# A batched trace of matrix products on one core: the first load as two transfers, 16 partitions issued by ScalarE and 112 by SyncE, without a critical section

## The chip, the core and the metric

The kernel runs on one core of a Trainium2 chip. The metric is the device time of one execution in microseconds (us). Before the change it is 706.29 us, the median of three runs (706.15 to 706.38).

The engines are named as in the profile: PE is TensorE (PEld its weight loads), DVE is VectorE, ACT is ScalarE, POOL is GpSimd, SP is SyncE. A transfer is issued by one of ACT, SP or POOL and carried out by the core's 16 DMA engines. Only the transfers that POOL issues change the type on the way (float32 in memory to bfloat16 in SBUF).

## What is computed

```python
prod = np.matmul(a, b)                                  # a, b: 8 x 2176 x 2176, float32
traces = np.diagonal(prod, axis1=1, axis2=2).sum(axis=-1)
```

The trace of a product needs no product: it is the sum over i and j of a[i, j] times b[j, i]. So the kernel has to read both inputs once, 303 MB, turn each `a` over, multiply it element by element with `b` and add up.

## The kernel before

The rows of a matrix are cut in three groups: two of 6 x 128 rows (`a_six`, `b_six`) and one of 5 x 128 rows (`five`). In a group, partition p holds 6 (or 5) neighbouring rows, one behind the other, so each partition is filled by one long contiguous read. For each of the 8 matrices of the batch:

- POOL issues the loads with `fetch` (L168-169): the five rows of `a` (L206), its twelve rows (L209), then the five and twelve rows of `b` (L218, L221). Each waits for the buffer that it writes to. The last matrix of `b` comes in ten pieces (L223 to L226).
- SP waits for the loads of `a` to land and passes this on to PE (the semaphore `moved`, L181 to L190).
- PE transposes 128 x 128 blocks into three PSUM slots (L344, L347); ACT (L236) and DVE (L265) copy them to `at` in SBUF.
- DVE multiplies `at` with the rows of `b` and reduces (L248). For the last matrix PE takes four of the seventeen column blocks (L314, L320), and the ends are added up at L352 and L295.

The first matrix starts in another way. Of the five rows per partition of `a[0]`, the first two (`FIRST` at L39, 4352 float32 elements per partition) are loaded as they are, by a transfer that ACT issues (L172), into memory that belongs to `b_six` and is free at that time (`words`, L166). ACT waits for it (L229) and rounds it to bfloat16 (L230). The other three of the five rows come by POOL's first transfer (L176), the twelve rows by its second (L177). PE starts when POOL's first transfer has landed and the rounding is done (L182 to L185).

ACT's transfer stands in a critical section of the tile framework (L171). On ACT that puts a no-operation, two branches, a semaphore update and a drain around the transfer, and SP waits for its end. Behind it `tc.close()` (L173) ends the framework's part of the program with barriers over all five engines, and only behind these come POOL's transfers and everything else. Another barrier of all five engines stands at the program's start, ahead of the section (L374 in the profile).

Of the kernel before, what the change touches and what calls it, by code (L numbers as in the profile page):

```python
# [22 lines left out]
def kernel(  # L23
# [7 lines left out]
    P = 128  # L31
# [3 lines left out]
    SIX, FIVE = 6, 5  # L35
    TWICE = 2 * SIX
    assert TWICE + FIVE == NT
    LAST = BATCH - 1
    FIRST = 2  # L39
# [76 lines left out]
    def flat(t):  # L116
        return t.rearrange("p r k -> p (r k)")
# [4 lines left out]
    def rows_of(src, start, m, r0, r1):  # L122
        return src[start:start + P * m, :].rearrange("(p r) k -> p (r k)", r=m)[:, r0 * N:r1 * N]
# [21 lines left out]
    def counted(name):  # L145
        return Counted(nc, name)
# [5 lines left out]
    d_a12, d_row = counted("load_a12"), counted("load_row")  # L152
# [12 lines left out]
    gp, act, sp, dve, pe = nc.gpsimd, nc.scalar, nc.sync, nc.vector, nc.tensor  # L165
    words = flat(b_six[:, 0:2 * FIRST, :].bitcast(f32))  # L166
# [1 line left out]
    def fetch(count, dst, src):  # L168
        count.by(gp.dma_start(out=dst, in_=src), 16)  # L169

    with tc.tile_critical(sync_engine=act.engine, no_gpsimd_drain=True):  # L171
        d_row.by(act.dma_start(out=words, in_=rows_of(a[0], TWICE * P, FIVE, 0, FIRST)), 16)  # L172
    tc.close()  # L173
    tc.compile()  # L174

# [20 lines left out]
    for n in range(BATCH):  # L196
        if n == 0:
            gp.wait_ge(zeros.sem, 2)
            for t in (identity32, identity16):
                ready.by(gp.affine_select(  # L200
                    out=t, in_=t, compare_op=mybir.AluOpType.not_equal, fill=1.0, base=0,
# [24 lines left out]
            fetch(d_late[k], piece.dst, piece.src)  # L226


    act.wait_ge(d_row.sem, 16)  # L229
    rounded.by(act.copy(out=flat(five[:, 0:FIRST, :]), in_=words))  # L230
    with nc.Fori(0, BATCH, engines=OrderedEngineSet([act.engine])):
        act.wait_ge(clear, 1).then_inc(clear, -1)  # L232
# [22 lines left out]
    with nc.Fori(  # L255
# [24 lines left out]
        for k, piece in enumerate(pieces[:len(whole) + 1]):  # L280
            if piece is whole[-1]:
                dve.wait_ge(parts.sem, k)
                parts.by(dve.reduce_sum(
                    out=sums[:, taken:taken + 1], in_=late[:, 0:k], axis=mybir.AxisListType.X,
# [11 lines left out]
            out=result[:1, :], in_=total.rearrange("o (b n) -> o b n", n=TAKEN),  # L296
# [5 lines left out]
    with nc.Fori(0, 2, engines=alone) as turn:  # L302
# [54 lines left out]
        out=out.rearrange("(a b) -> a b", a=1), in_=result[:1, :],  # L357
# [32 lines left out]
```

## Time and profile before

| what | before |
|---|---|
| median of three runs | 706.29 us |
| the profiled execution's own time | 706.07 us |
| its span, first to last instruction | 704.7 us |
| granted TensorE clock, mean | 0.647 |
| read from memory, over the span | 303.04 MB, 430 GB/s |
| busy share PE, DVE, ACT, POOL | 29%, 54%, 29%, 4% |
| transfers issued by POOL, share of the 16 DMA engines' span | 99.6% |
| transfer issued by ACT, the same share | 0.8% |

The span leaves out 1.37 us of the execution's own time (706.07 less 704.7), before its first and behind its last instruction. The profiled execution was 0.22 us below the median of the three runs. In the profile a DMA "packet" is one contiguous row of a transfer; a further packet of 4 bytes, one for each DMA engine that took part, counts up the transfer's semaphore. The size of a packet is what it writes: for the transfers of POOL half of what it reads. The share of a DMA queue is the time that its packets took, over 16 engines times the stretch that is looked at. A packet counts where it starts, so short stretches can show a little over 100%.

### The profile page before, as it was taken

What the parts mean: (1) busy time and instruction counts of PE and PEld (TensorE: products, weight loads), DVE (VectorE), ACT (ScalarE), POOL (GpSimd) and SP (SyncE); (2) the same over time, 40 slices, a digit from 0 to 9 for tenths busy, and PEclk for the clock granted to TensorE, in tenths of its full rate; (3) what the DMA queues carried; (4) which work ended last, traced back from release to release, by engine and by line L of the source; (5) the groups of instructions that cost most, each with busy time, mean ns of one, the idle gap of its engine ahead of it and who ended that gap; (6) DMA issues with size and microseconds to landing.
All of it is one profiled execution on the core that took longest, in us unless ns stands there. A gap on an engine that the chain in (4) does not pass through costs nothing. (4 is left out here: it accounts for less than half of the span.)

```text
span 704.7 us, 3807 instructions
## 1 busy us (share of the span) xinstructions
PE 205.4 (29%) x1573; PEld 181.8 (26%) x1573; DVE 382.8 (54%) x101; ACT 207.5 (29%) x162; POOL 25.6 (4%) x47
## 2 busy tenths in 40 slices
PE   0335012450124401344012440134301253014633
PEld 0324012440124401243012430134301243014522
DVE  0105487154871539616397163962639616396388
ACT  2427002470034600346004360044500445005900
POOL 1000000000000000000000000000000000001100
PEclk9759555795567855568556695567855678556955
DMA  9999999999999999999999999999999999999998
GB/s 252 230 200 219 215 228 213 217 225 213 206 216 217 223 213 229 213 213 214 224 209 213 215 228 209 224 222 209 209 229 213 213 211 232 206 215 224 218 206 174
DMA packets 7844, 152.66 MB, mean 217 GB/s; under 512 B 674, under 2 KB 930, under 8 KB 1442
## 3 DMA queue, kind: packets, MB, share of 16 engines
q0 software_dynamic: 7696, 150.41, 99.6%
q10 hardware_dynamic: 144, 2.23, 0.8%
q8 instruction: 1, 0.02, 0.0%
q14 instruction: 1, 0.01, 0.0%
q1 hardware_dynamic: 2, 0.00, 0.0%
HBM read 303.04 MB, written 0.00 MB: 430 GB/s over the span
## 5 line engine op out<-in xcount | busy, mean ns | idle before, releaser
L236 ACT COPY at<-aT 128x1536 bf16<-128x1536 bf16 (+3 forms) x160 | 202.4, 1360 | 452.0 <-ACTq L232 357.9
L248 DVE CUSTOM_DVE_ANT_0 at<-at,rows_b 128x10880 bf16<-128x10880 bf16 (+3 forms) x18 | 278.6, 15484 | 98.1 <-DMA rows_b<-in_b_dram 83.2
L265 DVE COPY at<-aT 128x1536 bf16<-128x1536 bf16 (+1 forms) x48 | 80.1, 1669 | 213.8 <-PE aT L344 163.4
L344 PE MATMUL aT<-identity,rows_b 128*128 128x128 f32 x240 | 54.3, 415 | 369.8 <-PEq L337 282.3
L344 PEld LDWEIGHTS aT<-identity,rows_b 128*128 128x128 f32 x240 | 46.3, 220 | 376.1 <-issue 283.1
L344 PE MATMUL aT<-identity,a_six 128*128 128x128 f32 x576 | 90.7, 320 | 94.9 <-SPq L190 80.8
L344 PEld LDWEIGHTS aT<-identity,a_six 128*128 128x128 f32 x576 | 83.6, 206 | 101.3 <-issue 90.1
L347 PE MATMUL aT<-identity,a_six 128*128 128x128 bf16 x480 | 34.3, 221 | 10.5 <-ACT at L236 9.4
L347 PEld LDWEIGHTS aT<-identity,a_six 128*128 128x128 bf16 x480 | 29.4, 119 | 15.0 <-ACT at L236 13.0
L169 POOL DMA_DIRECT2D rows_b<-in_b_dram x24 | 14.2, 614 | 333.1 <-PE aT L347 333.1
L248 DVE CUSTOM_DVE_ANT_1 at<-at,rows_b 128x3328 bf16<-128x3328 bf16 (+2 forms) x4 | 23.0, 5790 | 5.7 <-DMA rows_b<-in_b_dram 5.7
L314 PE MATMUL trace<-rows_b,at 128*128 x64 | 11.4, 286 | 20.0 <-PEq L311 20.0
L347 PE MATMUL aT<-identity,rows_b 128*128 128x128 bf16 x200 | 16.1, 251 | 0.0
L347 PEld LDWEIGHTS aT<-identity,rows_b 128*128 128x128 bf16 x200 | 15.9, 129 | 0.6 <-DVE at L265 0.2
L169 POOL DMA_DIRECT2D rows_b<-in_a_dram x8 | 4.6, 576 | 295.6 <-DVE sums L248 293.2
L314 PEld LDWEIGHTS trace<-rows_b,at 128*128 x64 | 6.7, 104 | 24.7 <-issue 22.9
L169 POOL DMA_DIRECT2D a_six<-in_a_dram x9 | 6.1, 675 | 0.0
L230 ACT CAST rows_b<-rows_b 128x4352 bf16<-128x4352 f32 x1 | 3.8, 3818 | 6.9 <-DMA rows_b<-in_a_dram 6.9
L230 ACT ACT_TABLE_LOAD x1 | 1.3, 1283 | 2.3 <-PEq L174 2.3
L320 PE MATMUL trace<-rows_b,at 128*128 128x128 bf16 x10 | 1.4, 309 | 0.8 <-DMA rows_b<-in_b_dram 0.7
L248 DVE DVE_READ_ACCUMULATOR2_ANT sums<- 128x1 f32 x17 | 1.4, 83 | 0.0
L241 DVE MEMSET ones<- 128x1 f32 x1 | 0.1, 59 | 2.4 <-PEq L174 2.4
(17 smaller groups left out, 4.2 us busy)
## 6 DMA issues: line engine op xcount, KB each, us to landing
a_six<-in_a_dram POOLq DMA_DIRECT2D x7, 6528.0 KB, 54.8
rows_b<-in_b_dram POOLq DMA_DIRECT2D x7, 6528.0 KB, 52.4
rows_b<-in_b_dram POOLq DMA_DIRECT2D x8, 2720.0 KB, 22.0
rows_b<-in_a_dram POOLq DMA_DIRECT2D x7, 2720.0 KB, 24.5
a_six<-in_a_dram POOLq DMA_DIRECT2D x2, 3264.0 KB, 46.7
rows_b<-in_a_dram ACTq DMA_DIRECT2D x1, 2176.0 KB, 9.5
rows_b<-in_b_dram POOLq DMA_DIRECT2D x1, 2176.0 KB, 31.5
rows_b<-in_b_dram POOLq DMA_DIRECT2D x2, 1088.0 KB, 38.4
```

Source lines behind the costliest of these rows:

```text
L169: count.by(gp.dma_start(out=dst, in_=src), 16)
L230: rounded.by(act.copy(out=flat(five[:, 0:FIRST, :]), in_=words))
L236: ins = act.copy(out=dst, in_=view(slots[t % SLOTS]))
L241: ready.by(dve.memset(ones, 1.0))
L248: return dve.tensor_tensor_reduce(out=x if out is None else out, in0=x, in1=y, scale=1.0, scalar=0.0, op0=MUL, op1=ADD, accum_out=acc,)
L265: ins = dve.tensor_copy(out=dst, in_=view(slots[t % SLOTS]))
L314: pe.matmul(trace_ps, x[:, block], y[:, block], start=False, stop=False)
L320: ins = pe.matmul(trace_ps, x[:, block], y[:, block], start=False, stop=piece.lo == 0 and c + P == piece.hi,)
L344: last = pe.transpose(ps[:, place, :], src, identity32)
L347: last = pe.transpose(ps16[:, place * P:(place + 1) * P], src, identity16)
```

## The change

The critical section goes. The rows of the same first load are cut by partitions in two transfers, both straight behind the program's first barrier: partitions 0 to 15 on ACT, partitions 16 to 127 on SP. Each is the first instruction of its engine in the framework's part of the program. Each is also taken out of the framework's own semaphore bookkeeping (`no_tile_sem_insts`). Both count up the same semaphore, so that ACT waits for 32 in place of 16 before it rounds. Nothing else differs; all lines behind stand three lower (L230 is now L233).

```diff
-    with tc.tile_critical(sync_engine=act.engine, no_gpsimd_drain=True):
-        d_row.by(act.dma_start(out=words, in_=rows_of(a[0], TWICE * P, FIVE, 0, FIRST)), 16)
+    first_rows = rows_of(a[0], TWICE * P, FIVE, 0, FIRST)
+    for engine, part in ((act, slice(0, 16)), (sp, slice(16, P))):
+        load = engine.dma_start(out=words[part], in_=first_rows[part])
+        tc.no_tile_sem_insts.add(load.ins.name)
+        d_row.by(load, 16)
     tc.close()
     tc.compile()
...
-    act.wait_ge(d_row.sem, 16)
+    act.wait_ge(d_row.sem, d_row.count)
     rounded.by(act.copy(out=flat(five[:, 0:FIRST, :]), in_=words))
```

This is the start of ACT's program before the change. The row of L172 is the first load, and the rows of L171 and L174 belong to the section and to the framework's end (drains and semaphore waits are not listed).

```order
L385 UNCONDITIONAL_BRANCH
L171 NO_OP
L174 UNCONDITIONAL_BRANCH
L172 DMA rows_b<-in_a_dram 128x4352
L171 UNCONDITIONAL_BRANCH
L171 NO_OP
L174 UNCONDITIONAL_BRANCH
L230 ACT_TABLE_LOAD
L230 CAST rows_b<-rows_b 128x4352
```

And this is the start of ACT's program with the change.

```order
L388 UNCONDITIONAL_BRANCH
L173 DMA rows_b<-in_a_dram 16x4352
L177 UNCONDITIONAL_BRANCH
L233 ACT_TABLE_LOAD
L233 CAST rows_b<-rows_b 128x4352
```

ACT's transfer has moved up past the section's first no-operation and branch, has 16 rows in place of 128, and is followed by one branch in place of two.

This is all that SP's program lists with the change. Before it there was no transfer between the first branch and the framework's end; the last row is the store of the result.

```order
L388 UNCONDITIONAL_BRANCH
L173 DMA rows_b<-in_a_dram 112x4352
L177 UNCONDITIONAL_BRANCH
L359 DMA out_dram<-result 1x8
```

SP now issues 112 of the 128 rows, ahead of the framework's end. POOL's program differs in one branch only: its two first transfers stand behind the same barriers as before.

## The prediction

> **What bounds the kernel.** I read the page's slices and queues first, to see whether any engine is short of work or the transfers are.
>
> ```profile
> DMA  9999999999999999999999999999999999999998
> ...
> DMA packets 7844, 152.66 MB, mean 217 GB/s; under 512 B 674, under 2 KB 930, under 8 KB 1442
> ...
> q0 software_dynamic: 7696, 150.41, 99.6%
> q10 hardware_dynamic: 144, 2.23, 0.8%
> ...
> q1 hardware_dynamic: 2, 0.00, 0.0%
> HBM read 303.04 MB, written 0.00 MB: 430 GB/s over the span
> ```
>
> The DMA engines are busy in every slice, while no other engine is above 54%. The queue q0 holds POOL's transfers, q10 is ACT's first load, q1 the store of the result by SP. To see whether there are holes smaller than a slice, I asked the DMA view for the stretch from 15 to 701 us.
>
> ```profile
> q0 software_dynamic: 7364, 148.62, 101.0%
> ```
>
> One packet at a time on each of 16 engines would make 100%, so there is no hole in 686 us. The issue table says why none opens: POOL is far ahead.
>
> ```profile
> rows_b<-in_b_dram POOLq DMA_DIRECT2D x7, 6528.0 KB, 52.4
> ```
>
> These loads write 6528 KB and read twice that, 13.4 MB, which takes 30.9 us at the stream's rate (303.04 MB from the first packet at 1.99 us to the last landing at 701.8 us: 433 GB/s). They land 52.4 us after their issue, so each lies some 21 us in the queue behind others. A load that is issued a microsecond earlier or later changes nothing by itself. Last comes the chain of waits, in order of time.
>
> ```profile
> 649.26 4.15 POOL rows_b L169 x8
> 653.41 48.37 DMA rows_b<-in_b_dram
> ...
> 701.83 0.84 PE trace L320 x6
> ...
> 703.34 0.18 DVE result L295
> ```
>
> The end is the last piece of `b`, and a fixed tail of 2.9 us behind it (704.7 less 701.8). So the time is the start of the stream, plus what 16 engines need for their packets one after another, plus that tail. Every engine's share is fixed by the program, so the slowest engine decides, and **time that an engine loses in the first load is never made up**: it comes back one to one at the end. That is the rule by which I price the change, and the change touches nothing but the first load.
>
> **The first load as it is.** The timeline shows the issues and what follows.
>
> ```profile
> 0.98 0.38 ACTq L172 DMA_DIRECT2D rows_b<-in_a_dram  x1
> 2.33 1.28 ACT L230 ACT_TABLE_LOAD   x1 [2.33 <-PEq L174]
> ...
> 2.83 0.67 POOL L169 DMA_DIRECT2D rows_b<-in_a_dram  x1 [2.38 <-POOLq L174]
> ...
> 10.51 3.82 ACT L230 CAST rows_b<-rows_b 128x4352 bf16<-128x4352 f32 x1 [6.90 <-DMA rows_b<-in_a_dram]
> 16.38 4.61 PEld L344 LDWEIGHTS aT<-identity,rows_b 128*128 128x128 f32 x25 [16.38 <-issue]
> ```
>
> The DMA view for 1.9 to 3 us has 40 slices of 0.0275 us; the fourth is the first with a packet, so the stream begins at 1.99, 1.01 us after ACT's issue began.
>
> ```profile
> DMA  0009000999099900090000000000000900000000
> ...
> DMA packets 16, 0.28 MB, mean 253 GB/s; under 512 B 0, under 2 KB 0, under 8 KB 0
> ...
> q10 hardware_dynamic: 16, 0.28, 114.7%
> ```
>
> These are 16 packets, the first row of each DMA engine: 114.7% of 1.1 us is 1.26 us for each. The view for 3.7 to 6.9 us shows the same queue once it runs.
>
> ```profile
> q10 hardware_dynamic: 80, 1.39, 102.2%
> ```
>
> That is 102.2% of 3.2 us x 16 engines for 80 packets: 0.65 us for a row of 17,408 bytes, 26.6 GB/s per engine and 426 GB/s for all. Eight rows per engine make 5.2 us, and the first costs 0.6 us more.
>
> **Term 1, the stream starts earlier.** Of ACT's old start at 0.98, the part ahead of the transfer inside the section goes. SP's waits show from when an engine is free behind the first barrier, and that the framework's end waited for ACT's section:
>
> ```profile
> SPq L174 <- ACTq L171: 0.9, 1, 0.9
> ...
> SPq L374 <- PEq L374: 0.7, 1, 0.7
> ```
>
> SP is let go at 0.7 us. Both transfers can begin at 0.74 or so, 0.24 us earlier. A smaller transfer may also deliver its first packet sooner. The nearest row is the store at the end, one row of 32 bytes: issued at 703.55 for 0.31 us, and in the DMA view from 703 to 704.7 its packets stand in slice 31 of 0.0425 us, at 704.28.
>
> ```profile
> 703.55 0.31 SPq L356 DMA_DIRECT2D out_dram<-result  x1
> ...
> GB/s 0 0 0 0 386 0 0 0 0 0 0 0 0 0 0 0 0 0 0 0 0 0 0 0 0 0 0 0 0 0 1 0 0 0 0 0 0 0 0 0
> ```
>
> That is 0.73 us to the first packet, against 1.01 with 128 rows. With 16 rows I take 0.81, so ACT's rows start at 1.55: **-0.44 us**. The bounds are -0.24 (1.01 us again) and -0.55 (0.70 plus 0.73 is 1.43). SP's 112 rows follow at about 1.75, inside ACT's first row, so no engine waits for them.
>
> **Term 2, ACT's 16 rows.** Before, each engine's eight rows were part of one transfer over all 128 partitions. Now one of the eight belongs to a transfer into partitions 0 to 15 alone, and all 16 engines write into these 16 partitions at the same time. No row of this trace shows a load of fewer than 128 partitions, so I bound it. If the width doesn't matter, the round takes 0.65 us as before: nothing lost. If 16 partitions take only their eighth of what 128 were seen to take (426 / 8 = 53 GB/s), the 278,528 bytes need 5.2 us: 4.6 us lost, since the row above shows one packet at a time per engine, and the engine can't do something else meanwhile. Below nothing there is no gain: the bytes and the rows per engine are the same. The nearest row, the first load itself, speaks for neither end: at eight rows per engine in step it wrote 3.3 GB/s per partition, and the end without a loss asks for 26.6 GB/s of each, which nothing here shows. I take the middle, 2.9 us: **+2.25 us**. [...]
>
> **Term 3, SP's 112 rows.** Seven per engine take 4.6 us at 0.65, as they did; at seven eighths of the rate 5.2. I take the middle, **+0.3 us** (0 to +0.65).
>
> **At no cost.** POOL's first transfers are issued earlier, since the end of the framework's part no longer waits 0.9 us for ACT's section but for two issues of 0.31 to 0.38 us from 0.74 on; I put POOL at 2.3 to 2.4 in place of 2.83. That hides a danger: POOL's packets come late behind their issue. The DMA view from 2 to 7 us holds a single one:
>
> ```profile
> q10 hardware_dynamic: 109, 1.90, 98.5%
> q0 software_dynamic: 1, 0.01, 1.2%
> ```
>
> So up to 4.1 us pass from issue to first packet, and the first load has to keep the engines busy until then. Its rows last from 1.55 to at least 7.3 (0.6 and eight times 0.65), POOL's come at 6.5 at the latest: covered, and without cover it would cost the difference. ACT's table load (1.28 us) and the wait of the rounding for 32 in place of 16 lie inside the 6.9 us that ACT waits for the load. PE starts at 16.38 when POOL's three rows have landed; the rounding ends 2 us before that (10.51 and 3.82 make 14.33). Queued behind the waiting ACT are only the copies of L236, and these wait for PE. A start that is some 2 us later shifts PE, and the 21 us in POOL's queue cover that. SP's transfer delays its `sem_inc`s by some tenths, and nobody asks for them before PE starts.
>
> **The sum.** -0.44 + 2.25 + 0.3 = +2.1 us. The profiled execution took 706.07 (span 704.7 and 1.37 around it), so 708.2; the median of the runs lies 0.22 above it, and on it the sum is **708.4 us**. With term 2 a quarter or three quarters of the way between its ends, the others as taken, it is 707.3 to 709.6: that is this forecast's own range.
>
> **Rivals.**
>
> *Width is free.* A DMA engine and not the place that it writes to sets the 0.65 us. For it: POOL's packets write only half of what they read, and the stream still reads 433 GB/s, as the first load does with 426; the limit seems to be on the reading side. Against it: that says nothing of 16 engines on 16 partitions. Terms 2 and 3 fall away and the start is kept: 705.85 us, not slower. It decides where ACT's rows take under about 1.3 us each beyond the first packet's extra 0.6.
>
> *The start does not move.* If the first packet is held at 1.99 by something other than the section, and width is free, nothing changes: 706.3. The row of the store, 0.73 us from issue to packet, speaks against it.
>
> *Fewer engines.* The 144 packets of q10 are 128 rows and 16 counts, so 16 engines; q1 shows 2 for one row, so one engine. If a 16-row transfer went to one engine, this one would have 15 rows more, 9.8 us: some 715.6. [...]
>
> *SP's rows are narrow too.* If the 16 engines fill 16 neighbouring partitions in each of SP's seven rounds, each round costs term 2 again: 7 x 2.25 more, 724.
>
> **How the numbers follow.** My forecast gets 0.60, width is free 0.31, the start does not move 0.03, and the two last ones 0.03 each. I predict 708.4. The range goes from 705.6, to take in most of the second case (705.85, less 0.1 to 0.2 if the start gains all that it can), to 709.6. Outside are the two last rivals with 0.06, the forecast above 709.6 with 0.05 and the second case below 705.6 with 0.05. A measurement of this kernel tells about 0.2%, 1.4 us, from no change, so slower means above 707.7: 0.50 of my 0.60 and the two last rivals, 0.56. Faster means under 704.9 and asks for a gain of 1.4 us, more than the 1.29 us by which the stream could start earlier if it began at 0.70: 0.01. The rest, 0.43, is within.
>
> **What would show it.** The first packet should stand at 1.5 to 1.6 (term 1), ACT's queue should hold 32 packets (16 rows, 16 counts) and SP's 128 more than before. Term 2 is the mean packet of ACT's queue: about 3.5 us (2.9 and the extra 0.6) if I am right, about 1.26 if width is free. Term 3 is the mean packet of SP's queue, 0.65 to 0.74. POOL's queue from 15 us on should still read 101%, with the last landing 2 us later. A hole there, or a first load over 15 us long, would mean that I have the wrong mechanism.

## The result, and the profile after

The changed kernel takes 709.73 us, the median of six runs (709.36 to 710.12), against 706.23 for six runs of the kernel before: 3.50 us or 0.5% slower, ratio 1.005 with the interval [1.004, 1.006]. The profiled execution took 710.12 us (span 708.7), 0.39 above the median and the slowest of the six, so differences that are read in its trace come out some tenths larger.

These are the page's lines on the transfers. Columns of the queues: packets, megabytes written, share of 16 engines' span.

```profile
DMA  9999999999999999999999999999999999999998
...
q0 software_dynamic: 7696, 150.41, 99.0%
q1 hardware_dynamic: 130, 1.95, 1.2%
q10 hardware_dynamic: 32, 0.28, 0.2%
...
HBM read 303.04 MB, written 0.00 MB: 428 GB/s over the span
```

The bytes are the same. The first load took 0.8% of the span on ACT's queue; now it takes 1.4% on two. The 32 packets of q10 are 16 rows and 16 counts, and q1 has 128 more than the 2 of the store: each of the two transfers ran on all 16 DMA engines.

For the same stretch of both kernels, 1.7 to 23 us, the DMA view of the kernel before shows

```profile
q0 software_dynamic: 208, 3.34, 73.4%
q10 hardware_dynamic: 144, 2.23, 27.6%
```

and that of the changed kernel

```profile
q0 software_dynamic: 179, 2.59, 57.0%
q1 hardware_dynamic: 128, 1.95, 39.2%
q10 hardware_dynamic: 32, 0.28, 6.6%
```

27.6% of 21.3 us is 5.9 us on each engine for the first load before; 45.8% is 9.8 us now. These 3.9 us are most of the difference. With the stream 0.24 us earlier they make 3.6, while the chain below ends 4.1 us later (PE's last products start at 705.94 against 701.83). The shares are means over 16 engines, and the slowest engine decides; where the last 0.5 us lie, these views don't show. Behind the first load nothing has changed, as the same view for 20 to 701 us of the changed kernel shows: no hole,

```profile
q0 software_dynamic: 7021, 147.50, 101.0%
```

and the chain of waits ends with the same pieces.

```profile
656.46 48.81 DMA rows_b<-in_b_dram
...
705.94 0.84 PE trace L323 x6
...
707.45 0.18 DVE result L298
```

The start is in the timeline of the changed kernel.

```profile
0.74 0.41 ACTq L173 DMA_DIRECT2D rows_b<-in_a_dram  x1
0.74 0.38 SPq L173 DMA_DIRECT2D rows_b<-in_a_dram  x1
1.91 1.28 ACT L233 ACT_TABLE_LOAD   x1 [1.91 <-PEq L177]
...
2.41 0.67 POOL L169 DMA_DIRECT2D rows_b<-in_a_dram  x1 [1.96 <-POOLq L177]
...
15.64 3.82 ACT L233 CAST rows_b<-rows_b 128x4352 bf16<-128x4352 f32 x1 [12.45 <-DMA rows_b<-in_a_dram]
20.51 4.56 PEld L347 LDWEIGHTS aT<-identity,rows_b 128*128 128x128 f32 x22 [20.51 <-issue]
```

Both issues begin at 0.74, 0.24 earlier than ACT's did, and POOL comes at 2.41 in place of 2.83. But the rounding starts 5 us later (15.64 against 10.51), and PE 4 us later (20.51 against 16.38). Which rows moved first is in the DMA view from 1.7 to 3 us (slices of 0.0325 us):

```profile
DMA  0990990009990000900000900000000000090090
...
q1 hardware_dynamic: 16, 0.28, 88.8%
q10 hardware_dynamic: 3, 0.05, 17.4%
```

The second slice has the first packet, at 1.75. All 16 first rows are SP's; ACT's, issued at the same time, come second, the first of them in the 36th slice, at 2.84. The view from 2.8 to 3.7 us has all of ACT's rows, the one from 3.7 to 5.8 us SP's second rows:

```profile
q10 hardware_dynamic: 16, 0.28, 153.5%
```

```profile
q1 hardware_dynamic: 16, 0.28, 89.4%
```

153.5% of 0.9 us is 1.38 us for a row of ACT, and 89.4% of 2.1 us is 1.88 us for the row of SP behind it. Ahead of the change a row took 0.65. Between them these two lost 2.0 us, and more of it in SP's row than in ACT's: the row that takes longer need not be the one whose transfer is to blame, and only runs without one of the two can tell. The rest of the 3.9 is in SP's other rows; over the whole load SP's rows took 1.19 us each (39.2% of 21.3 us on 16 engines, for 112 rows).

POOL's packets begin only at 9.2 us (the view from 2 to 9.2 us has none), 6.8 us behind the issue. The engines stayed busy even so. From 6.8 to 15 us the two queues that move data make 102.5%:

```profile
q1 hardware_dynamic: 83, 1.20, 55.9%
q0 software_dynamic: 62, 0.81, 46.6%
```

### The profile page after: what moved, and what is told of

Its sections match the earlier page's. It is cut to its first block, busy times and chain, and to the rows that moved or that the text cites. A ratio compares the mean times of both kernels' runs of the same rounds, so it can differ in the third digit from the quotient of the medians.

```text
span 708.7 us, 3800 instructions
## 1 busy us (share of the span) xinstructions
PE 206.5 (29%) x1573; PEld 183.0 (26%) x1573; DVE 382.8 (54%) x101; ACT 207.5 (29%) x162; POOL 25.6 (4%) x47
## 5 line engine op out<-in xcount | busy, mean ns | idle before, releaser
L251 DVE CUSTOM_DVE_ANT_0 at<-at,rows_b 128x10880 bf16<-128x10880 bf16 (+3 forms) x18 | 278.6, 15484 | 98.4 <-DMA rows_b<-in_b_dram 83.6
L233 ACT CAST rows_b<-rows_b 128x4352 bf16<-128x4352 f32 x1 | 3.8, 3817 | 12.5 <-DMA rows_b<-in_a_dram 12.5
```

The source lines that it names most:

```text
L251: return dve.tensor_tensor_reduce(out=x if out is None else out, in0=x, in1=y, scale=1.0, scalar=0.0, op0=MUL, op1=ADD, accum_out=acc,)
```

## The experiments

All change the first load alone. Theory W: the cut is the cause, because it changes which partitions the 16 DMA engines write into at the same time. Against it stood Q (two queues), S (no critical section), R (the order in which memory is read), and, for a detail, O (the place of the 16 rows in the order) and I (two issuers).

**The change without its cut.**

```diff
-    for engine, part in ((act, slice(0, 16)), (sp, slice(16, P))):
+    for engine, part in ((sp, slice(0, P)),):
```

> One transfer of all 128 partitions, issued by SyncE as its first instruction, no critical section, nothing on ScalarE: the change without its cut. [...] Theory S (leaving the section, and with it issuing before the framework's end, costs the time): 709 or more.

Measured: 705.97 us against 706.21, ratio 0.9998 [0.9989, 1.0008]. The loss is gone, and S falls. The median lies 0.24 us lower, just what the earlier issue gives, but the interval holds no change too. Its first load takes as long as before the change (view from 1.7 to 23 us: 27.7% against 27.6%):

```profile
q1 hardware_dynamic: 144, 2.23, 27.7%
```

**Two issuers, cut by columns.**

```diff
-    for engine, part in ((act, slice(0, 16)), (sp, slice(16, P))):
-        load = engine.dma_start(out=words[part], in_=first_rows[part])
+    for engine, part in ((act, slice(0, 544)), (sp, slice(544, FIRST * N))):
+        load = engine.dma_start(out=words[:, part], in_=first_rows[:, part])
```

> Two issuers and two queues as in the change, ScalarE an eighth of the bytes and SyncE seven eighths, but cut by columns: each transfer spans all 128 partitions (544 and 3808 float32 of the 4352 in each). Theory W: no loss, 705.9 to 706.3. Theory Q: the loss stays, 709 to 710. Theory R (rows of neighbouring partitions read at the same time disturb each other in memory): no loss either, since each engine reads the rows that it read before.

Measured: 706.07 us, ratio 0.9996 [0.9986, 1.0006]. Two issuers, two queues and an eighth of the bytes on ACT, and no loss. Q falls; what is left of the change is the cut by partitions.

**The cut by partitions, one issuer.**

```diff
-    for engine, part in ((act, slice(0, 16)), (sp, slice(16, P))):
+    for engine, part in ((sp, slice(0, 16)), (sp, slice(16, P))):
```

> The change's cut of 16 and 112 partitions, but both issued by SyncE, one behind the other, on one queue. Theories W and R: the loss stays, 709 to 710.3, and the 16 rows come first. Theory Q: 706.0 to 706.3.

Measured: 708.72 us, ratio 1.0033 [1.0020, 1.0045]. Most of the loss stays on one queue, as W says, but it is 1.0 us smaller than with two issuers, and below the range that I gave. The last two experiments take that up.

**Only the 112 partitions.**

```diff
-    for engine, part in ((act, slice(0, 16)), (sp, slice(16, P))):
+    for engine, part in ((sp, slice(16, P)),):
...
+    act.wait_ge(zeros.sem, 4)
     act.wait_ge(d_row.sem, d_row.count)
...
     dve.memset(sums, 0.0)
+    zeros.by(dve.memset(words[0:16], 0.0))
```

> Only the 112 partitions are loaded, by SyncE; partitions 0 to 15 of the first two rows are set to zero by VectorE and not read at all (so 0.28 MB less is read, worth 0.65 us). My prediction had the loss in ScalarE's 16 rows (2.25 of 2.55 us): then 705.35 plus 0.3, 705.4 to 706.0. If the trace of the changed kernel reads rightly, with SyncE's rows at 1.19 us each, most of the loss is in the 112 rows: 707 to 708.5. [...]

Measured: 707.45 us, inside what the trace of the changed kernel had suggested. This kernel leaves out the 16 rows; with the 0.65 us that they would take, it is 708.10, or 2.13 us above the uncut load (705.97). My prediction had 0.3 for this. Its trace agrees (view from 1.7 to 23 us):

```profile
q1 hardware_dynamic: 128, 1.95, 35.0%
```

35.0% of 21.3 us is 7.5 us on each engine. The uncut load took 5.9, or 5.2 without one row of 0.65, so 2.2 us are lost. SP's 112 rows are more than half of the loss, and the 16 rows add 1.63 to them (709.73 less 708.10).

**The crowding by itself: eight transfers of 16 partitions.** A two by two: into 16 neighbouring partitions or into every eighth, reading neighbouring rows or every eighth.

```diff
-    for engine, part in ((act, slice(0, 16)), (sp, slice(16, P))):
-        load = engine.dma_start(out=words[part], in_=first_rows[part])
+    near, far = lambda k: slice(16 * k, 16 * k + 16), lambda k: slice(k, P, 8)
+    for k in range(8):
+        load = (act, sp)[k % 2].dma_start(out=words[near(k)], in_=first_rows[near(k)])
```

The first has `near` for both, the second `near` for the partitions and `far` for the rows, the third `far` and `near`, the fourth `far` for both.

> The disputed cost alone and large: the first load in eight transfers of 16 neighbouring partitions, in turn on ScalarE and SyncE, each reading the 16 neighbouring rows that belong there. [...] If it sits in the uneven seven rows per engine of the 112, there is no loss here: 706 to 707.

> Eight transfers into 16 neighbouring partitions as in the kernel before this one, but each reads every eighth row of the source (the rows arrive in the wrong partitions, so part of the first matrix is mixed up; the bytes are the same). [...] Theory R: fast, or as the kernel with distant partitions and distant rows.

> Eight transfers into every eighth partition, each reading 16 neighbouring rows of the source (again rows in the wrong partitions, the same bytes). [...] Theory R: as slow as neighbouring partitions with neighbouring rows.

> Eight transfers into every eighth partition, each reading the rows that belong there. [...] Theory R: no loss, 706 to 707. If a width of 16 partitions costs whatever they are, as slow as neighbouring partitions.

Measured, one execution each (the kernel before: 706.21):

| partitions | rows read | us |
|---|---|---|
| neighbours | neighbours | 719.45 |
| neighbours | every eighth | 717.21 |
| every eighth | neighbours | 710.61 |
| every eighth | every eighth | 711.10 |

The partitions that are written decide: 6 to 9 us, whatever is read. R doesn't explain the loss; what is read makes 2.2 us in one pair and -0.5 in the other, a side effect that single executions don't settle. Over the kernel before, neighbours cost 13.24 and 11.00 us, every eighth partition 4.40 and 4.89. Both fit W, which gives no sizes by itself. The DMA view from 4 to 14 us of the first of the four shows rows and counts in turn:

```profile
DMA packets 140, 1.22 MB, mean 122 GB/s; under 512 B 70, under 2 KB 70, under 8 KB 70
...
q10 hardware_dynamic: 70, 0.61, 49.3%
q1 hardware_dynamic: 70, 0.61, 49.1%
```

98.4% of 10 us on 16 engines for 70 rows is 2.25 us a row in place of 0.65, and 122 GB/s in place of 426. In the last of the four, from 4 to 11 us:

```profile
DMA packets 170, 1.53 MB, mean 219 GB/s; under 512 B 82, under 2 KB 82, under 8 KB 82
...
q1 hardware_dynamic: 84, 0.80, 53.7%
q10 hardware_dynamic: 86, 0.73, 50.0%
```

103.7% of 7 us for 88 rows is 1.32 us a row, twice 0.65. So 16 engines on 16 neighbours ran at between a quarter and a third of their rate (122 of 426 GB/s), on every eighth partition at half (219 of 426). What in the hardware makes neighbours slower is not shown by these runs.

**Halves.**

```diff
-    for engine, part in ((act, slice(0, 16)), (sp, slice(16, P))):
+    for engine, part in ((act, slice(0, 64)), (sp, slice(64, P))):
```

> The common cut: partitions 0 to 63 by ScalarE, 64 to 127 by SyncE, each as first instruction. [...] Theory that only an uneven number of rows (seven) costs: 706.

Measured: 710.42 us, ratio 1.0059 [1.0042, 1.0075]. The common cut has the highest median of the cuts in two, 4.45 us over the uncut load. The two halves were not even under way at the same time: the DMA view from 1.7 to 6.8 us lists SP's 64 rows and nothing else, and the one from 6.8 to 15 us has ACT's 64 rows, with ten of its counts.

```profile
q1 hardware_dynamic: 64, 1.11, 101.7%
```

```profile
q10 hardware_dynamic: 74, 1.11, 57.1%
```

101.7% of 5.1 us on 16 engines is 1.30 us a row: a single transfer into 64 neighbouring partitions, with no other beside it, ran at half the rate (0.65 us a row before the change), like those into every eighth partition (1.32). So the loss needs neither a second queue under way nor many transfers. What two halves would take if they ran together, this run can't tell. A smaller part of the 4.45 is the start, for a reason that isn't shown: the first packet stands in the twelfth slice of the view from 1.7 to 3 us, at 2.07 in place of 1.77 for the uncut load.

```profile
DMA  0000000000099909990090000000009000000090
```

**The order of the two transfers.** One issuer with the 112 rows ahead:

```diff
-    for engine, part in ((act, slice(0, 16)), (sp, slice(16, P))):
+    for engine, part in ((sp, slice(16, P)), (sp, slice(0, 16))):
```

> One issuer as before (SyncE, cut of 16 and 112, where the 16 rows went first and the time was 708.72), but the 112 rows first and the 16 last. Theory O (the 16 rows are cheap only as an engine's first packet, where the slow first delivery covers part of their crowding): 709.4 to 710.2, as with two issuers. Theory I (two issuers cost 1.0 us by themselves): 708.7 again.

Two issuers with ACT's 16 rows ahead:

```diff
-    for engine, part in ((act, slice(0, 16)), (sp, slice(16, P))):
-        load = engine.dma_start(out=words[part], in_=first_rows[part])
-        tc.no_tile_sem_insts.add(load.ins.name)
-        d_row.by(load, 16)
+    load = act.dma_start(out=words[0:16], in_=first_rows[0:16])
+    tc.no_tile_sem_insts.add(load.ins.name)
+    d_row.by(load, 16)
     tc.close()
     tc.compile()
+    d_row.by(sp.dma_start(out=words[16:P], in_=first_rows[16:P]), 16)
```

> Two issuers as in the change, but SyncE issues its 112 rows only behind the framework's end, about 1.1 us later, so that ScalarE's 16 rows are the first packet of each engine. Theory O: 708.7 to 709.0. Theory I: 709.7 or, with a gap between the first and second row of some engines, up to 710.

Measured: 710.06 us (ratio 1.0048 [1.0032, 1.0065]) with the 16 rows last, 708.80 (1.0036 [1.0024, 1.0049]) with them first. So I falls and O holds: it is the place in the order, whoever issues (the four runs with the 16 rows last spread from 709.22 to 710.35, so second and last place are not told apart). Over the 112 rows alone (708.10) the 16 rows cost 0.6 and 0.7 us as first packets, 1.6 in the change, where they come second, and 2.0 as last. That the slow first delivery (1.26 us for a first row before the change, against 0.65 for a later one) covers a part of the crowding fits this; the trace doesn't show the cover by itself.

The DMA view from 1.7 to 3 us of this last kernel also tells whether a small transfer delivers sooner (slices of 0.0325 us):

```profile
DMA  0099990990990000000000009000000010000000
...
q10 hardware_dynamic: 20, 0.28, 113.2%
```

Issued at 0.74 and alone, the 16 rows have their first packet in the third slice, at 1.77. So have the 128 rows of the uncut load in the same view:

```profile
DMA  0099099909900000090009090000000000000000
...
q1 hardware_dynamic: 16, 0.28, 98.8%
```

Their issue is SP's first instruction, as in the changed kernel, where it began at 0.74 too. So 16 rows were no sooner than 128.

## Why the prediction was wrong

The sign held, and half of the mechanism: the load is slower because of the cut by partitions, and a loss in the first load comes back at the end. But I put nearly all of the loss on ACT's 16 rows, and more than half of it is on SP's 112. The sum was 3.50 against 2.1, and 709.73 lies 0.13 above the range. That it is no further off is luck: term 3 was 1.8 us short and term 1 gave 0.2 too much gain, while term 2, 0.6 too dear, hid a part of that. The terms below are differences of the same medians, so that they add up to 3.5 is no test of them.

- **Time that is lost in the first load is never made up: right.** 3.9 us more per engine in the load and 0.24 less at the start, about 4 us later at the end in the profiled execution; 0.5 of that is not accounted for. The uncut load loses nothing and the time is back at 705.97.
- **Term 1, -0.44: too large, -0.24.** The issue moved by 0.24 as worked out. The 0.20 that a 16-row transfer should have brought, read from the store of one row, did not come: 1.0 us from issue to packet for 16 rows as for 128. The store goes the other way, and its 0.73 did not carry over to a load. Nor did ACT's rows come first.
- **Term 2, +2.25: roughly right, 1.6.** That the middle of such wide bounds came near is partly luck. In the eight transfers into neighbours a round costs 1.6 us more than a wide one (2.25 less 0.65), and at the end of the load 2.0. The sign that I gave for this term misled: ACT's mean packet was 1.38 us, near the 1.26 that I had put down for free width and far from 3.5, while SP's row behind it took 1.88.
- **Term 3, +0.3: the step that failed, 2.1.** I priced 112 partitions by their number, seven eighths of 128 and so nearly the full rate, and gave 0.65 to 0.74 us for SP's mean packet; it was 1.19, and 112 rows alone cost 2.13 us. The number of partitions is not what sets the rate: 16 neighbours and 16 spread partitions differ (2.25 and 1.32 us a row), and 64 neighbours are as slow as 16 spread ones (1.30). So what counts seems to be which partitions the 16 engines write into at the same moment. Why the seven rows per engine of the 112 cost so much more than the eight of the 128 is not shown: it may be the partitions that come together in them, or something else about seven rows. My last rival, that SP's rows are narrow too, named the fault, but for 16 neighbours in each round, far too much (724). How the rows are dealt out to the engines, and with it the cause of the 2.1, stays open.
- **At no cost: right.** POOL issued its first transfer at 2.41, as worked out. Its packets did not come by 6.5 "at the latest" but at 9.2; the first load was so much longer that there was no hole before them. PE's late start was covered by POOL's queue.
- *Width is free* is ruled out by the two by two; *the start does not move* by the first packet at 1.75 in place of 1.99; *fewer engines* by the packet counts.

## What to carry to other kernels

In a kernel whose DMA engines never rest, price a load by engine time per row, and cut it, if it must be cut, by columns: each part then still spans all 128 partitions (706.07, against 709.73 by 16 and 112 partitions and 710.42 by halves). One transfer from one issuer does as well, and what there was to gain here, the 0.24 us of an earlier issue, needs no cut: dropping the critical section and issuing the whole load from SyncE gives 705.97, 3.8 below the changed kernel; below the kernel before it is by less than these runs can tell from no change.

## What was not expected of the hardware

- A transfer into 112 of 128 partitions was already much slower than one into all: 2.1 us on rows that took 5.2.
- Two halves on two queues did not add up: 4.45 us slower than one whole. SP's half ran first, all 64 rows of it, and ACT's behind it, though both were issued at 0.74.
- Of two transfers issued within 0.01 us, SP's 112 rows had all 16 first packets and ACT's 16 rows all second ones (1.75 and 2.84 us).
